# Spreading rows of cumulated decays over the partitions: transfers from DRAM in place of selecting matmuls, in a hybrid SSD and gated DeltaNet block

## The chip, the cores and the metric

The kernel runs on one core of one Trainium2 chip. The metric is the device time of one execution in microseconds. One execution was taken by the hardware profiler; all rows in this text come from that one. Engines are named as the profile names them: PE is the matmul engine, PEld its weight load, DVE the vector engine, ACT the scalar engine, POOL GpSimd, SP the sync engine, which here issues nearly all transfers (SPq is its sequencer).

## The reference, cut to what matters

One residual layer: an input projection feeds two token mixers (a Mamba-2 SSD and a gated DeltaNet), which are merged by gates and followed by a SwiGLU FFN. Both mixers work chunk by chunk and weigh pairs of tokens of a chunk by the decay between them:

```python
def segsum_exp(a_cum):
    l = a_cum.shape[-1]
    mask = jnp.tril(jnp.ones((l, l), dtype=bool))
    diff = a_cum[..., :, None] - a_cum[..., None, :]
    return jnp.exp(jnp.where(mask, diff, -jnp.inf))
...
scores = cb[:, :, :, None] * segsum_exp(a_cum)                           # SSD, 32 heads in 4 groups
qk = jnp.einsum("bchlk,bchsk->bchls", q, k) * decay                      # DeltaNet, 16 value heads
a_low = jnp.where(strict, jnp.einsum("bchlk,bchsk->bchls", k_beta, k) * decay, 0.0)
```

So for each head and chunk a square of exp(a_cum[l] - a_cum[s]) is wanted. The kernel works on 1040 tokens (16 meta tokens and 1024 others) in eight chunks of 128, and a ninth chunk, number 8, that holds the 16 meta tokens.

## The kernel before, in words

**Stages.** The norm and the first tiles of the projection come first (to about 105 us of the profile). Then eight DeltaNet subproblems of two value heads each run (to about 1090 us), then four SSD groups of eight heads (to about 1740 us), then the branch projections, the output projection and the FFN. While the mixers run, the PE also does the rest of the input projection: tiles of 128 columns by `dense` (L138, each step three matmuls on L141 to L143), with the weights loaded and split by `load_w` (L130). A tile that passes a convolution is copied to `raw` (L378); a gate or z tile is evacuated by ACT into `zt`, a tile with three buffers (L394, L408).

**The decays.** `cum` holds, with tokens on the partitions, the cumulated log decay of 48 heads (32 of the SSD, 16 of the DeltaNet). The square of a chunk needs the same numbers as a row that lies along the free dimension and is the same on all 128 partitions. The kernel makes it in two steps. At the start (L355 to L370) `cum` is transposed into `rr`, three copies of 32 heads below one another, and each copy is cut into three bfloat16 parts, which stand in `rowD` and `rowS`. Later `decay` (L416) does one matmul per head (L420): a column of the selecting matrix `selD` or `selS`, read by all output columns, times `row`, so that the three parts are added in PSUM on every partition. ACT then takes the difference to `cum` with a Relu per head (L423) and one Exp for all heads of the call (L426).

**Who calls it.** In a DeltaNet subproblem `i`, `dn_p1` (L501) runs for nine chunks: PE makes the product of the keys (L510), `decay` fills `E` for two heads, DVE masks the product (`kkm`, L513) and multiplies (L516) into `W`. After chunks 3 and 7 eight transfers each store `W` to `nd` (L523). `dn_inv` (L528) loads it as `X`, inverts it on DVE (L539, L541), stores and loads it again. `dn_merge` (L554, first matmuls L563) and `dn_p2` (L600) follow, chunk by chunk; `dn_p2` calls `decay` for a tile `E2`, which meets the PE again in L641. `E` and `E2` have two buffers each, from a pool with `bufs=2`. In the SSD, `ssd_chunk` (L690) calls `decay` twice for four heads, into tiles `Es` (three buffers) used by the matmuls of L748; each call has a PSUM bank of its own, of tag "p", from which ACT also takes `ec` (L733).

**What sets the order.** The kernel is written for a scheduler that puts each engine's instructions, SP's transfers among them, in an order of their readiness, with those that come earlier in the program first. It isn't the order of the program: in the profile matmuls of L141 to L143 stand between those of `dn_merge` and `dn_p2`. A tile of a tag waits for a buffer of that tag. The PSUM tag "p" has two banks; `dn_merge`, `dn_p1` and `ssd_chunk` take theirs from it.

Of the kernel before, what the change touches and what calls it, by code (L numbers as in the profile page):

```python
# [10 lines left out]
F32 = mybir.dt.float32  # L11
# [10 lines left out]
NM = 16  # L22
# [70 lines left out]
def body(tc, A):  # L93
# [77 lines left out]
    rs_dram = [dram.tile([8, 128], F32, name=f"rs_{g}") for g in range(NGRP)]  # L171
    nd_dram = [dram.tile([66, 32, 32], F32, name=f"nd_{i}") for i in range(NSUB)]
# [51 lines left out]
    rowS = tkp.tile([96, TT], BF16, name="rowS")  # L224
    rowD = tkp.tile([96, TT], BF16, name="rowD")
    selS = tkp.tile([96, 32], BF16, name="selS")
    selD = tkp.tile([96, 16], BF16, name="selD")
# [61 lines left out]
    with tc.tile_pool(name="dab", bufs=1) as sb:  # L289
# [4 lines left out]
        s0 = sb.tile([96, 48], F32, name="s0")  # L294
        sp.dma_start(s0, A["c_sel"])
        dve.tensor_copy(selS, s0[:, 0:32])
        dve.tensor_copy(selD, s0[:, 32:48])
# [57 lines left out]
        for row, h0 in ((rowD, 16), (rowS, 0)):  # L355
            c3 = sb.tile([128, 9, 3, 32], F32, name="c3")
            pool.tensor_copy(c3, cum[:, :, h0:h0 + 32].unsqueeze(2).broadcast_to([128, 9, 3, 32]))
            rr = sb.tile([96, TT], F32, name="rr")
            b2 = sb.tile([96, TT], BF16, name="b2")
            for c in range(9):  # L360
                c0, L = (NM + 128 * c, 128) if c < 8 else (0, NM)
                ps = psm("p")
                pe.transpose(ps[0:96, 0:L], V(c3[0:L, c], "p a b -> p (a b)"), ident[0:L, 0:L])
                act.copy(rr[:, c0:c0 + L], ps[0:96, 0:L])
            for i in range(3):
                r32 = slice(32 * i, 32 * i + 32)
                act.copy(row[r32], rr[r32])
                if i < 2:
                    dve.tensor_copy(b2, rr)
                    dve.tensor_tensor(rr, rr, b2, op=ALU.subtract)  # L370
# [44 lines left out]

    def decay(E, ps, row, sel, h0, hs, c):  # L416

        c0, L = cr(c)
        for i, h in enumerate(hs):
            pe.matmul(ps[0:L, 128 * i:128 * i + L], sel[:, h:h + 1].broadcast_to([96, L]),  # L420
                      row[:, c0:c0 + L], start=True, stop=True)
        for i, h in enumerate(hs):
            act.activation(E[0:L, i, 0:L], ps[0:L, 128 * i:128 * i + L], AF.Relu,  # L423
                           bias=cum[0:L, c, h0 + h:h0 + h + 1], scale=-1.0)
        n = len(hs)
        act.activation(E[0:L, 0:n, 0:L], E[0:L, 0:n, 0:L], AF.Exp, scale=-1.0)  # L426

# [73 lines left out]
    def dn_p1(i, c):  # L501
# [9 lines left out]
        decay(E, ps, rowD, selD, 32, (2 * i, 2 * i + 1), c)  # L511
# [88 lines left out]
    def dn_p2(i, c):  # L600
# [11 lines left out]
        decay(E, ps, rowD, selD, 32, (2 * i, 2 * i + 1), c)  # L612
# [77 lines left out]
    def ssd_chunk(g, c):  # L690
# [35 lines left out]
        E = [sb2.tile([128, 4, 128], F32, name="Es", bufs=3) for _ in range(2)]  # L726
        for q in range(2):
            pd = psm("p")
            decay(E[q], pd, rowS, selS, 0, range(8 * g + 4 * q, 8 * g + 4 * q + 4), c)
            pd = V(pd, "p (a b l) -> p a b l", a=2, b=2)  # L730
            for b in range(2):
                r = slice(64 * b, 64 * b + 64)
                act.activation(ec[r, 2 * q:2 * q + 2], pd[r, :, b], AF.Exp)  # L733
            dve.tensor_tensor(E[q], E[q], cbm.unsqueeze(1).broadcast_to([128, 4, 128]), op=ALU.mult)
# [439 lines left out]
def prepare(inp):  # L1174
# [46 lines left out]
    sel = z(96, 48)  # L1221
    for i in range(3):
        sel[32 * i:32 * i + 32, 0:32] = np.eye(32)
        sel[32 * i + 16:32 * i + 32, 32:48] = np.eye(16)
    d["c_sel"] = sel
    return d


# [11 lines left out]
```

## Time and profile before

| | us |
|---|---|
| median of 3 runs | 2960.96 |
| lowest and highest of them | 2960.52, 2972.54 |
| the profiled execution, its own time | 2960.07 |
| its span, first to last instruction | 2958.4 |
| mean granted clock of the PE | 0.99 of full |

The profile has a page with the busy time of each engine, the time that each group of instructions took, and the chain of work that ended last; the trace answers for single stretches, lines and tiles. Busy time of the PE is modelled for pipelined matmuls, so two matmuls that overlap can both be long: what one costs is the distance between the starts of its neighbours.

### The profile page before, as it was taken

The page shows a single profiled execution, that of the slowest core. Times are in us where ns is not written, and L with a number is a line of the kernel's source. Part 1 is how long each engine was busy: PE and PEld are TensorE (multiplying, and loading weights), DVE is VectorE, ACT ScalarE, POOL GpSimd, SP SyncE. Part 2 cuts the span into 40 slices and gives each one's busy share as a digit, 9 for nine tenths or more (in the row PEclk, how much of TensorE's full clock was granted, in tenths as well). Part 3 has the DMA queues.
Part 4 walks back from the last instruction along what each step waited for, and adds up shares of the span by engine and source line. Part 5 has one row for each costly group of instructions (what it writes and reads, how often), then busy time and mean ns, then how long its engine had stood idle before and what let it go on. Part 6 is the DMA issues. An engine that isn't in the chain of part 4 may idle for free.

```text
span 2958.4 us, 42844 instructions
## 1 busy us (share of the span) xinstructions
PE 2900.6 (98%) x16121; PEld 2442.0 (83%) x16121; DVE 1971.9 (67%) x3882; ACT 1293.4 (44%) x3240; POOL 184.8 (6%) x193
## 2 busy tenths in 40 slices
PE   8999999999999999999999999999997999999997
PEld 7888888888888889979888778888876788888886
DVE  7678687787786755767777753564768655556446
ACT  5645545546456353545555544122234233333213
POOL 1000000000000000000000000000101432230000
PEclk9999999999999999999999999999998999999998
DMA  3111121120111201011111124352442222226212
GB/s 114 51 51 44 41 61 44 37 65 27 53 58 30 93 29 51 30 67 47 51 45 45 68 76 154 106 178 90 135 160 86 102 83 86 86 85 224 90 54 75
DMA packets 119255, 227.33 MB, mean 77 GB/s; under 512 B 47064, under 2 KB 53880, under 8 KB 119048
## 3 DMA queue, kind: packets, MB, share of 16 engines
q1 hardware_dynamic: 117320, 222.50, 22.7%
q8 instruction: 127, 2.08, 0.3%
q10 hardware_dynamic: 1728, 2.10, 0.2%
q14 instruction: 80, 0.66, 0.1%
HBM read 175.16 MB, written 49.38 MB: 76 GB/s over the span
## 4 chain that ended last, share of the span: by engine, by line
PE 91%; DVE 4%; DMA 2%; issue 1%; ACT 1%; POOL 1%; SPq 0%; DVEq 0%; ACTq 0%; POOLq 0%
PE psd L142 16%; PE psd L141 16%; PE psd L143 16%; PE pq_p L1002 1%; PE pq_p L1003 1%; PE ps_o L748 1%; PE pq_p L1004 1%; PE ps_p L563 1%; PE pq_psd L1002 1%; PE ps_o L641 1%; PE ps_z L448 1%; PE pq_psd L1003 1%; PE pq_psd L1004 1%; PE ps_a L631 1%; PE ps_b L738 1%
## 5 line engine op out<-in xcount | busy, mean ns | idle before, releaser
L142 PE MATMUL psd<-u_lo,whi 128*128 128x512 f32 (+3 forms) x2136 | 766.2, 359 | 3.7 <-DVE u_lo L150 2.7
L141 PE MATMUL psd<-u_hi,whi 128*128 128x512 f32 (+3 forms) x2136 | 761.1, 356 | 0.0
L143 PE MATMUL psd<-u_hi,wlo 128*128 128x512 f32 (+3 forms) x2136 | 754.9, 354 | 0.7 <-DVE wlo L135 0.7
L134 ACT CAST whi<-wraw 128x1024 fp32r<-128x1024 f32 (+2 forms) x197 | 188.0, 954 | 634.8 <-PE psd L142 454.3
L142 PEld LDWEIGHTS psd<-u_lo,whi 128*128 128x128 f32 x2136 | 406.2, 190 | 40.5 <-issue 5.1
L143 PEld LDWEIGHTS psd<-u_hi,wlo 128*128 128x128 f32 x2136 | 403.9, 189 | 33.0 <-issue 3.3
L141 PEld LDWEIGHTS psd<-u_hi,whi 128*128 128x128 f32 x2136 | 402.6, 189 | 34.6 <-issue 4.2
L135 DVE TENSOR_TENSOR wlo<-wraw,whi 128x1024 fp32r<-128x1024 f32 (+2 forms) x197 | 217.8, 1106 | 138.8 <-ACT whi L134 129.5
L143 PE MATMUL psd<-blk,wlo 128*128 128x512 f32 x512 | 199.4, 389 | 0.8 <-DVE wlo L135 0.8
L141 PE MATMUL psd<-blk,whi 128*128 128x512 f32 x512 | 199.2, 389 | 0.0
L142 PE MATMUL psd<-blk,whi 128*128 128x512 f32 x512 | 199.2, 389 | 0.0
L143 PEld LDWEIGHTS psd<-blk,wlo 128*128 128x128 f32 x512 | 96.1, 188 | 21.6 <-DVE wlo L135 1.7
L141 PEld LDWEIGHTS psd<-blk,whi 128*128 128x128 f32 x512 | 96.1, 188 | 20.0
L142 PEld LDWEIGHTS psd<-blk,whi 128*128 128x128 f32 x512 | 96.1, 188 | 19.8
L908 DVE TENSOR_TENSOR part<-part,psd 128x512 f32<-128x512 f32 x96 | 65.5, 683 | 70.2 <-PE psd L143 70.2
L378 ACT COPY raw<-psd 128x256 f32<-128x256 f32 x165 | 73.4, 445 | 81.9 <-PE psd L143 80.1
L379 POOL MEMSET raw<- 128x3 f32 x56 | 6.3, 113 | 1393.0 <-DVE qk L384 537.1
L986 POOL TENSOR_TENSOR sw<-wraw 128x512 f32<-128x512 f32 x44 | 69.3, 1575 | 353.1 <-DMA wraw<-w_gu 345.1
L702 DVE TENSOR_TENSOR xdt<-ps_z,dtb 128x512 f32<-128x512 f32 (+1 forms) x36 | 24.8, 690 | 89.0 <-PE ps_z L699 89.0
L539 DVE TENSOR_TENSOR itmp<-X 66x30 f32<-66x30 f32 (+14 forms) x240 | 78.2, 326 | 6.3 <-DMA X<-nd 0.8
L541 DVE TENSOR_TENSOR X<-X,itmp 66x30 f32<-66x30 f32 (+14 forms) x240 | 78.3, 326 | 5.9
L423 ACT ACTIVATE Es<-ps_p,cum 128x128 f32<-128x128 f32 x256 | 75.4, 371 | 11.0 <-PE ps_p L420 10.9
(678 smaller groups left out, 6145.3 us busy)
## 6 DMA issues: line engine op xcount, KB each, us to landing
wraw<-w_in SPq DMA_DIRECT2D x105, 512.0 KB, 3.3
wraw<-w_gu SPq DMA_DIRECT2D x48, 512.0 KB, 3.3
wraw<-w_br SPq DMA_DIRECT2D x36, 512.0 KB, 3.4
c<-hc SPq DMA_DIRECT2D x22, 512.0 KB, 2.6
hc<-c SPq DMA_DIRECT2D x22, 512.0 KB, 5.7
wraw<-w_dn SPq DMA_DIRECT2D x40, 256.0 KB, 2.6
g<-zt SPq DMA_DIRECT2D x32, 256.0 KB, 2.0
y_d<-zt SPq DMA_DIRECT2D x32, 256.0 KB, 2.1
```

The lines of the kernel that those rows point to most:

```text
L134: act.copy(hi[:, 0:kk], raw[:, 0:kk])
L135: dve.tensor_tensor(lo[:, 0:kk], raw[:, 0:kk], hi[:, 0:kk], op=ALU.subtract)
L141: pe.matmul(ps[:, 0:n], hi[:, wk0 + k], ahi(k), start=(k == 0), stop=False)
L142: pe.matmul(ps[:, 0:n], hi[:, wk0 + k], alo(k), start=False, stop=False)
L143: pe.matmul(ps[:, 0:n], lo[:, wk0 + k], ahi(k), start=False, stop=(k == kk - 1))
L378: dense_u((name, lambda ps, p0, p1: act.copy(raw[:, 3 + p0:3 + p1], ps)))
L423: act.activation(E[0:L, i, 0:L], ps[0:L, 128 * i:128 * i + L], AF.Relu, bias=cum[0:L, c, h0 + h:h0 + h + 1], scale=-1.0)
L539: dve.tensor_tensor(t, X[:, 0:j, j:j + 1].broadcast_to([66, j, m]), X[:, j:j + 1, j + 1:32].broadcast_to([66, j, m]), op=ALU.mult)
L541: dve.tensor_tensor(X[:, 0:j, j + 1:32], X[:, 0:j, j + 1:32], t, op=ALU.add)
L908: dve.tensor_tensor(part[:, m, cs], part[:, m, cs], ps, op=ALU.add)
L986: pool.tensor_tensor(t, x, y, op=op)
L1002: pe.matmul(ps, w[0][:, k], y[0][:, k], start=start and k == 0, stop=False, skip_group_check=not start)
```

## The change

The rows are no longer made by matmuls. At the start `cum` is transposed once for all 48 heads (nine transposes of 48 columns in place of eighteen of 96), copied to `rr` by ACT, and stored to a DRAM tensor `cum_dram` by one transfer. The bfloat16 parts and the selecting matrices go. A new function `spread` issues one transfer on SP per call of `decay`: it reads `n` rows of a chunk from `cum_dram` and writes them to every partition of the decay tile. `decay` then works in place in SBUF, with the same Relu per head and the same Exp. In the SSD the two transfers are issued ahead, `ec` is taken from the decay tile before `decay` overwrites it, no PSUM bank of tag "p" is used for it, and `Es` has four buffers in place of three.

```diff
-        for row, h0 in ((rowD, 16), (rowS, 0)):
-            c3 = sb.tile([128, 9, 3, 32], F32, name="c3")
-            pool.tensor_copy(c3, cum[:, :, h0:h0 + 32].unsqueeze(2).broadcast_to([128, 9, 3, 32]))
-            rr = sb.tile([96, TT], F32, name="rr")
-            b2 = sb.tile([96, TT], BF16, name="b2")
-            for c in range(9):
...
-                pe.transpose(ps[0:96, 0:L], V(c3[0:L, c], "p a b -> p (a b)"), ident[0:L, 0:L])
-                act.copy(rr[:, c0:c0 + L], ps[0:96, 0:L])
-            for i in range(3):
-                r32 = slice(32 * i, 32 * i + 32)
-                act.copy(row[r32], rr[r32])
-                if i < 2:
-                    dve.tensor_copy(b2, rr)
-                    dve.tensor_tensor(rr, rr, b2, op=ALU.subtract)
+        rr = sb.tile([48, TT], F32, name="rr")
+        for c in range(9):
...
+            pe.transpose(ps[0:48, 0:L], cum[0:L, c], ident[0:L, 0:L])
+            act.copy(rr[:, c0:c0 + L], ps[0:48, 0:L])
+        sp.dma_start(cum_dram, rr)
...
-    def decay(E, ps, row, sel, h0, hs, c):
+    def spread(E, h0, n, c):
 
         c0, L = cr(c)
-        for i, h in enumerate(hs):
-            pe.matmul(ps[0:L, 128 * i:128 * i + L], sel[:, h:h + 1].broadcast_to([96, L]),
-                      row[:, c0:c0 + L], start=True, stop=True)
-        for i, h in enumerate(hs):
-            act.activation(E[0:L, i, 0:L], ps[0:L, 128 * i:128 * i + L], AF.Relu,
-                           bias=cum[0:L, c, h0 + h:h0 + h + 1], scale=-1.0)
-        n = len(hs)
+        sp.dma_start(E[0:L, 0:n, 0:L], cum_dram[h0:h0 + n, c0:c0 + L].unsqueeze(0).broadcast_to([L, n, L]))
+
+    def decay(E, h0, n, c):
+
+        c0, L = cr(c)
+        for i in range(n):
+            act.activation(E[0:L, i, 0:L], E[0:L, i, 0:L], AF.Relu, bias=cum[0:L, c, h0 + i:h0 + i + 1], scale=-1.0)
         act.activation(E[0:L, 0:n, 0:L], E[0:L, 0:n, 0:L], AF.Exp, scale=-1.0)
...
-        decay(E, ps, rowD, selD, 32, (2 * i, 2 * i + 1), c)
+        spread(E, 32 + 2 * i, 2, c)
+        decay(E, 32 + 2 * i, 2, c)
...
-        E = [sb2.tile([128, 4, 128], F32, name="Es", bufs=3) for _ in range(2)]
+        E = [sb2.tile([128, 4, 128], F32, name="Es", bufs=4) for _ in range(2)]
         for q in range(2):
-            pd = psm("p")
-            decay(E[q], pd, rowS, selS, 0, range(8 * g + 4 * q, 8 * g + 4 * q + 4), c)
-            pd = V(pd, "p (a b l) -> p a b l", a=2, b=2)
+            spread(E[q], 8 * g + 4 * q, 4, c)
+        for q in range(2):
+            pd = V(E[q], "p (a b) l -> p a b l", b=2)
             for b in range(2):
                 r = slice(64 * b, 64 * b + 64)
                 act.activation(ec[r, 2 * q:2 * q + 2], pd[r, :, b], AF.Exp)
+            decay(E[q], 8 * g + 4 * q, 4, c)
             dve.tensor_tensor(E[q], E[q], cbm.unsqueeze(1).broadcast_to([128, 4, 128]), op=ALU.mult)
```

## Rows read from the trace of the kernel before

**Rows 1.** The page, busy time, share of the span and instructions by engine.
```profile
PE 2900.6 (98%) x16121; PEld 2442.0 (83%) x16121; DVE 1971.9 (67%) x3882; ACT 1293.4 (44%) x3240; POOL 184.8 (6%) x193
```

**Rows 2.** The page, shares of the span in the chain that ended last.
```profile
PE 91%; DVE 4%; DMA 2%; issue 1%; ACT 1%; POOL 1%; SPq 0%; DVEq 0%; ACTq 0%; POOLq 0%
```

**Rows 3.** Stretches: length, busy us (count) by engine, granted clock, DMA share, GB/s.
```profile
370.00:434.00 64.00, 63.88 (x387) 56.94 (x386) 57.88 (x135) 27.96 (x74) 1.40 (x5) 1.00 0.24 70
434.00:490.00 56.00, 56.00 (x412) 45.10 (x411) 38.92 (x136) 39.04 (x154) 0.10 (x1) 1.00 0.07 18
...
1190.00:1330.00 140.00, 140.00 (x861) 116.92 (x860) 101.43 (x165) 75.54 (x176) 0.51 (x5) 1.00 0.15 52
```

**Rows 4.** The same view of line 141 alone, its PE and PEld time.
```profile
434.00:490.00 56.00, 8.22 (x20) 3.60 (x19) 1.00 0.07 18
```

**Rows 5.** Line 420: count, ns min/median/max, first and last start us.
```profile
L420 PE MATMUL ps_p<-rowS,selS x256: 216/218/232, 1189.1 to 1734.1; 96*128 96x128 bf16 x128
L420 PE MATMUL ps_p<-rowD,selD x144: 169/217/222, 96.5 to 984.4; 96*128 96x128 bf16 x128, 96*16 96x16 bf16 x16
L420 PE MATMUL ps_b<-rowD,selD x128: 217/221/314, 105.4 to 1076.8; 96*128 96x128 bf16 x128
```

**Rows 6.** PE in order of time, SSD: start us, us, line, tiles, count.
```profile
1330.33 0.39 PE L420 MATMUL ps_p<-rowS,selS 96*128 96x128 bf16 x4
1330.56 1.11 PE L738 MATMUL ps_b<-Ct,Ss 128*128 128x128 f32 x8
...
1333.14 0.40 PE L142 MATMUL psd<-u_lo,whi 128*128 128x512 f32 x1
1333.37 0.40 PE L143 MATMUL psd<-u_hi,wlo 128*128 128x512 f32 x1
1333.69 0.38 PE L420 MATMUL ps_p<-rowS,selS 96*128 96x128 bf16 x4
1333.89 0.48 PE L141 MATMUL psd<-u_hi,whi 128*128 128x512 f32 x1
1334.20 0.40 PE L142 MATMUL psd<-u_lo,whi 128*128 128x512 f32 x1
```

**Rows 7.** PE in order of time, DeltaNet, around one pair of L420.
```profile
245.75 0.28 PE L420 MATMUL ps_p<-rowD,selD 96*128 96x128 bf16 x2
245.84 0.42 PE L141 MATMUL psd<-u_hi,whi 128*128 128x384 f32 x1
```

**Rows 8.** Groups by line and shape: busy us, mean ns, idle before by releaser.
```profile
L426 ACT ACTIVATE E<-E 128x256 f32<-128x256 f32 x128 | 53.6, 420 | 2.4
...
L423 ACT ACTIVATE E<-ps_p,cum 128x128 f32<-128x128 f32 x128 | 41.3, 367 | 12.5 <-PE ps_p L420 4.4 <-DVE W L516 3.0 <-DVE f L662 1.7
...
L516 DVE SCALAR_TENSOR_TENSOR W<-E,w,kkm 128x128 f32<-128x128 f32 x128 | 39.8, 344 | 2.0 <-ACT E L426 0.8
L651 ACT ACTIVATE oq<-v 128x128 f32<-128x128 f32 x128 | 37.9, 299 | 9.1 <-DVE v L647 7.2 <-DVE rrr L162 1.8
L449 ACT ACTIVATE ps_z<-ps_z 128x128 f32<-128x128 f32 x128 | 33.9, 265 | 32.1 <-PE ps_z L448 31.8
```

**Rows 9.** Transfers: count, KB each, median us to landing; last, all of rst.
```profile
nd<-W SPq DMA_DIRECT2D x128, 16.0 KB, 1.5
X<-nd SPq DMA_DIRECT2D x8, 256.0 KB, 3.7
...
rst<-rs SPq DMA_DIRECT2D x4, 512.0 KB, 5.9
...
DMA to landing us min/median/max: 4.6/5.9/5.9
```

**Rows 10.** SP in order of time, fifth subproblem: start us, us, transfer, count.
```profile
603.10 8.61 SPq L523 DMA_DIRECT2D nd<-W  x16
```

**Rows 11.** Line 516 between 580 and 725 us, the fifth subproblem's decays used.
```profile
L516 DVE SCALAR_TENSOR_TENSOR W<-E,w,kkm x16: 341/346/352, 596.4 to 608.2; 128x128 f32<-128x128 f32 x16
```

**Rows 12.** Line 641 between 434 and 490 us, eight chunks of one subproblem.
```profile
L641 PE MATMUL ps_o<-v,E x32: 270/275/377, 444.3 to 489.6; 128*128 128x128 f32 x32
```

More of the change, by code (lines that the diff above doesn't have):

```diff
@@ L171, in body @@
     rs_dram = [dram.tile([8, 128], F32, name=f"rs_{g}") for g in range(NGRP)]
+    cum_dram = dram.tile([48, TT], F32, name="cum_d")
     nd_dram = [dram.tile([66, 32, 32], F32, name=f"nd_{i}") for i in range(NSUB)]
@@ L223, in body @@
     dte = tkp.tile([128, 9, 48], F32, name="dte")
[L224 to L227, printed above, removed]
     convp = tkp.tile([128, len(CONV), 5], F32, name="convp")
@@ L293, in body @@
         dve.tensor_scalar(dnw, dnw, 0.5, None, op0=ALU.mult)
[L294 to L297, printed above, removed]
         alog = sb.tile([128, 48], F32, name="alog")
@@ L352, in body @@
         act.activation(dte, lastb, AF.Exp)
-        for row, h0 in ((rowD, 16), (rowS, 0)):
-            c3 = sb.tile([128, 9, 3, 32], F32, name="c3")
-            pool.tensor_copy(c3, cum[:, :, h0:h0 + 32].unsqueeze(2).broadcast_to([128, 9, 3, 32]))
-            rr = sb.tile([96, TT], F32, name="rr")
-            b2 = sb.tile([96, TT], BF16, name="b2")
-            for c in range(9):
-                c0, L = (NM + 128 * c, 128) if c < 8 else (0, NM)
-                ps = psm("p")
-                pe.transpose(ps[0:96, 0:L], V(c3[0:L, c], "p a b -> p (a b)"), ident[0:L, 0:L])
-                act.copy(rr[:, c0:c0 + L], ps[0:96, 0:L])
-            for i in range(3):
-                r32 = slice(32 * i, 32 * i + 32)
-                act.copy(row[r32], rr[r32])
-                if i < 2:
-                    dve.tensor_copy(b2, rr)
-                    dve.tensor_tensor(rr, rr, b2, op=ALU.subtract)
+        rr = sb.tile([48, TT], F32, name="rr")
+        for c in range(9):
+            c0, L = (NM + 128 * c, 128) if c < 8 else (0, NM)
+            ps = psm("p")
+            pe.transpose(ps[0:48, 0:L], cum[0:L, c], ident[0:L, 0:L])
+            act.copy(rr[:, c0:c0 + L], ps[0:48, 0:L])
+        sp.dma_start(cum_dram, rr)
     def conv_tile(name, out, raw=None):
@@ L611, in dn_p2 @@
         pe.transpose(ps[:, 384:512], kT, ident)
-        decay(E, ps, rowD, selD, 32, (2 * i, 2 * i + 1), c)
+        spread(E, 32 + 2 * i, 2, c)
+        decay(E, 32 + 2 * i, 2, c)
         qkm = sb.tile([128, 128], F32, name="qkm")
@@ L1220, in prepare @@
     d["c_stri"] = np.triu(np.ones((128, 128), np.float32), 1)
[L1221 to L1225, printed above, removed]
     return d
```

## The prediction

> **What bounds the kernel now.** I read the page's busy times first. The PE is busy for 2900.6 us, 98% of the span; DVE stands at 67%, ACT at 44% [rows 1]. Then the chain that ended last: the PE holds 91% of it, transfers 2% [rows 2]. So work taken from the PE is the likeliest to come back as time, and new transfers touch something that now hardly ends anything. Third, the stretches, since a mean over stages could hide others. In the SSD stretch from 1190 to 1330 us the PE has no idle time at all, and in the two DeltaNet stretches, 370 to 434 and 434 to 490, it is idle for 0.12 and 0.00 us [rows 3]. These two differ, though. In the first, in which one subproblem is inverted and the next convolutions run, DVE is busy for 57.88 of 64 us. In the second, in which `dn_merge` and `dn_p2` run, DVE has 38.92 of 56, and the PE spends only 20 steps (of three matmuls each) on the projection [rows 4]; the rest are small matmuls of a chain that goes from PE to ACT to DVE and back. There a busy PE is also a PE that fills the waits of a chain with projection work that happens to be ready. That is where this change can lose what it saves.
>
> The Trainium skill, Perfetto Trace Analysis, section Identifying the Most-Contended Engine, says that matmul busy time is a bad measure of the PE's load and that the share of LDWEIGHTS is a better one. This trace has 83% there [rows 1], so by that rule the PE has some slack, and part of the matmul time removed would not come back; the first rival below is that case.
>
> **What is removed from the PE.** 256 selecting matmuls of the SSD, 144 of `dn_p1` and 128 of `dn_p2`, 528 in all [rows 5]. Their median durations of 217 to 221 ns overlap and are not their price. The price is the distance between starts. Four in a train of small matmuls: from 1330.33 to 1330.56, 0.23 us. Four between projection matmuls: from the start of L143 at 1333.37 to that of L142 at 1334.20 are 0.83 us, in which two projection matmuls would take 2 x 0.23 (1333.14 to 1333.37), so 0.36 us [rows 6]. There are 64 fours in the SSD: 64 x 0.23 = 14.7 at least, 64 x 0.36 = 23.0 at most; both kinds are frequent, so I take 0.29 each, 18.6 us. In the DeltaNet they come in pairs, 136 of them. One pair takes 0.09 us from its start to the next projection matmul [rows 7]; half of a four in a train would be 0.115. I take 0.10: 13.6 us, with bounds of 0.09 and 0.12, 12.2 to 16.3. Nine fewer transposes at the start, at the 0.06 us that one of four takes in a train, give 0.5 us. Sum: 18.6 + 13.6 + 0.5 = 32.7 us less work on the PE, with bounds of 27 and 40.
>
> The start also loses bfloat16 casts and subtractions on ACT and DVE. I count them at nothing: the rows were ready at 96.5 us, when the first selecting matmul ran [rows 5], and what fills the time is the PE's projection work. For the same reason I count the new store of `cum_dram` and the wait of the first `spread` for it at nothing; both lie beside the projection.
>
> **What is added on ACT.** The Relu now reads SBUF. The nearest rows are one function, Square with accumulation, on 128x128: 265 ns from PSUM, 299 from SBUF [rows 8]. So 34 ns for each of 528 Relus and 128 `ec`s: 22 us over 1600 us. ACT is busy for 39.04 of 56 and 75.54 of 140 us [rows 3], so this is covered; if it weren't, it would lie on the chunk's chain with 0.1 us per chunk.
>
> **What is added on SP and the transfers.** 136 transfers of 128 KB (eight of them 16-wide) and 64 of 256 KB. No row shows one of this size that spreads rows over partitions. The nearest is `rst`, the same form with 512 KB: 4.6 to 5.9 us to landing. Below lies the 16 KB of `nd` with 1.5, beside it the 256 KB of `X` with 3.7 [rows 9]. A line between `nd` and `rst` gives 2.2 to 2.5 us for 128 KB and 3.0 to 3.6 for 256 KB. I take 2.4 and 3.3, with 1.5 and 3.7 as bounds for the first. The transfer waits for a buffer, so what matters is how far ahead it is issued.
>
> In the SSD, `Es` has four buffers, two chunks. The selecting matmuls of 32 chunks run from 1189.1 to 1734.1 us [rows 5], 17 us a chunk. A buffer comes free when a chunk's L748 is over, so the transfer for the chunk after the next has some 17 us, and needs 3.3, or 5.9 for both together. Hidden. SP's stores of `zt` and the weight loads are queued on the same engine: a `spread` that waits for its buffer delays the weight load behind it. But a load goes into the second of two `wraw` buffers, a whole tile ahead, so I count this at nothing. If that cover were gone, each transfer would cost its 3.3 us, 64 x 3.3 = 211 us in all; with 17 us a chunk nothing points that way.
>
> In `dn_p2`, the 32 matmuls on `E2` of eight chunks start between 444.3 and 489.6 us [rows 12], 5.7 us a chunk. The transfer for chunk c is issued when L641 of chunk c-2 is over, so 11 us remain. It needs 2.4 + 2 x 0.37 + 0.42 for Relus and Exp [rows 8], and some 0.4 on DVE: 4 us. Hidden.
>
> In `dn_p1` it is not. Two buffers of `E` come free by L516 of DVE, and the chunks follow one another closely: sixteen L516 of eight chunks start within 596.4 to 608.2 us [rows 11], 1.5 us a chunk, 13.7 us for nine. After the change the two first chunks are loaded early, since their buffers have long been free. The other seven go in two alternating lanes, at most four rounds one after the other. A round is the transfer, two Relus, the Exp and two L516: 2.4 + 0.73 + 0.42 + 0.69 = 4.2 us [rows 8]. Four make 17 us. The eight stores of `W` after chunk 3 hold SP for half of 8.61 us [rows 10], and the `spread` of chunk 5, free at the same moment, waits behind them: 4.3 more. So 21 us in place of 13.7 plus its start, about 6 us longer. With 1.5 us to landing and the spreads ahead of the stores it is 13 us, no longer than now; with 3.7 and the stores 26 us, 12.6 longer. Below nothing isn't expected: the first two chunks start a little earlier, but a lane can't be faster than its round.
>
> What of it ends up in the time? `dn_p1` is followed by the stores, `dn_inv` and `dn_merge`, one chain per subproblem; the PE goes on with the projection meanwhile. Its reserve: `zt` has three buffers, so three halves of eight steps, 24, can be run ahead of `dn_p2`'s end, and 20 are used now [rows 4]. The four left are twelve matmuls of 0.23, 2.8 us of cover. A second cover is in `dn_inv`: DVE works there on convolutions in between (57.88 of 64 us [rows 3]), and a later inversion finds more of these done; I put this at 2 us. So 6 - 2.8 - 2 = 1.2 us uncovered, for seven subproblems (the first waits for the start anyway): 8 us.
>
> **The sum.** Against the profiled execution, 2960.07 us, which is 0.9 below the median of the runs shown (too little to matter here): 2960 - 33 + 8 = 2935 us, a gain of 0.8%. Its own bounds are 2922 (40 saved, little lost) and 2946 (27 saved, 1.9 us uncovered per subproblem).
>
> **The rivals.**
> - *The chain, not the PE, bounds the DeltaNet.* Then the 13.6 us saved there don't come back, since the PE's small matmuls only fill a chain, and DVE gives no cover: 6 - 2.8 = 3.2 us for seven subproblems, 22 us. 2960 - 19 + 22 = 2963, no change. For it: only 20 projection steps in 56 us [rows 4] and PEld's 83%. Against it: idle PE time is nil in both stretches [rows 3].
> - *Slower, by the rounds of `dn_p1`.* A transfer that lands after 3.7 us makes the nine chunks 12.6 us longer. The reserve covers 2.8, the rest delays the inversion: 9.8 x 7 = 69 us. 2960 - 33 + 69 = 2996. It decides from the point at which the uncovered part of a subproblem passes 33 / 7 = 4.7 us. For it: X takes 3.7 us [rows 9], and weight loads share the queue. Against it: this stretch moves little, with a DMA share of 0.24 and 0.07 [rows 3].
> - *More gain.* The selecting matmuls cost 0.36 and 0.12 everywhere and nothing is lost: 2960 - 40 = 2920. For it: `dn_p1` and the SSD hold PSUM banks of tag "p" for a shorter time. Against it: four in a train cost 0.23 [rows 6].
>
> **How the numbers follow.** The forecast gets 0.60, no change 0.22, slower 0.13, more gain 0.05. The likeliest is 2935. The range from 2920 to 2978 holds the forecast, the first rival and the end of more gain; it leaves out the slower one and a little beyond. A measurement of this kernel can tell about 0.5%, 15 us, from no change. Faster by more than that: 0.60 + 0.05 = 0.65; within: 0.22; slower: 0.13.
>
> **What would show it.** Right: line 420 gone and the count of PE matmuls down by about 540; the SSD stage shorter by about 18 us with the PE still without idle time; the chain of the end with hardly any transfer of `cum`; landing near 2.4 and 3.3 us. For the loss: the span of L516 in a subproblem, 12 us now, near 18, and PE idle time of some 1 us before `dn_merge` or L641. Wrong: ACT waits at L423 for transfers in the SSD, PE idle time at L748, weight loads that come late behind a `spread`, or a span of L516 that passes 22 us.

## The result: slower by 4%, and the profile after

| | before | after |
|---|---|---|
| median, us | 2961.86 (4 runs, 2960.52 to 2972.54) | 3081.36 (4 runs, 3077.11 to 3088.74) |
| ratio, 95% interval | | 1.040, 1.037 to 1.043 |
| profiled execution, its span, us | 2960.07, 2958.4 | 3082.38, 3080.5 |
| DeltaNet, us (from 105 us to the end of its last L641 / L627) | 984.1 | 1050.4 |
| SSD, us (from there to the end of its last L748 / L735) | 649.0 | 707.2 |
| rest, us | 1220.3 | 1217.9 |

The forecast was a gain of 26 us; the change lost 120. Two stages lost it, 66 and 58 us; the rest, which the change doesn't touch, stayed. The split between the two is not clean: in its longer DeltaNet stage the PE also did projection work that before was left to the SSD stage (next rows). In the code of after the numbers are: `spread` L403, Relu L409, Exp L410 (before L423, L426), the products of `dn_p1` L501 (L516), `ec` L719 (L733), the matmuls on `Es` L735 (L748), those on `E2` L627 (L641).

The page of after: busy times and the chain that ended last, which answer to [rows 1, 2], then two groups (busy, mean ns, idle before and its releaser).

```profile
PE 2911.3 (95%) x15584; PEld 2440.1 (79%) x15584; DVE 1966.6 (64%) x3872; ACT 1314.0 (43%) x3225; POOL 178.6 (6%) x191
...
PE 75%; DMA 10%; ACT 7%; DVE 5%; issue 3%; POOL 0%; SPq 0%; DVEq 0%; ACTq 0%; POOLq 0%
...
L409 ACT ACTIVATE E<-E,cum 128x128 f32<-128x128 f32 (+1 forms) x272 | 94.8, 389 | 66.9 <-DMA E<-cum_d 65.8
L719 ACT ACTIVATE ec<-Es 64x256 f32<-64x256 f32 x128 | 52.9, 413 | 153.6 <-DMA Es<-cum_d 152.0
```

The PE has 537 matmuls fewer (528 selecting ones and nine transposes) and yet is busy for 10.7 us more. Transfers, 2% of the chain before, are 10% of it now, and ACT stood for 152.0 us before `ec` and 65.8 us before Relus of the DeltaNet until rows had landed. So the forecast's sign that something is wrong, waits of ACT for transfers in the SSD, is there. The three stages of after and then of before (length, busy us and count of PE, PEld, DVE, ACT, POOL, then the granted clock, DMA share, GB/s):

```profile
105.00:1155.00 1050.00, 997.80 (x6138) 838.58 (x6137) 739.36 (x2061) 533.09 (x1736) 10.09 (x41) 0.97 0.24 62
1155.00:1863.00 708.00, 644.51 (x3737) 554.28 (x3736) 461.89 (x751) 352.54 (x752) 2.21 (x22) 0.96 0.33 70
1863.00:3080.00 1217.00, 1173.93 (x5207) 967.69 (x5205) 689.46 (x962) 367.58 (x592) 148.84 (x102) 0.98 0.34 112
```

```profile
105.00:1089.00 984.00, 982.57 (x6336) 832.49 (x6336) 739.83 (x2061) 528.25 (x1772) 11.53 (x46) 0.99 0.16 49
1089.00:1738.00 649.00, 648.81 (x4078) 561.01 (x4076) 459.03 (x752) 336.18 (x756) 2.23 (x22) 1.00 0.15 52
1738.00:2958.00 1220.00, 1174.06 (x5210) 968.12 (x5208) 689.18 (x963) 367.72 (x592) 151.63 (x102) 0.98 0.33 112
```

The PE is now idle for 52 of 1050 us and 63 of 708 us, where it had been idle for 1.4 and 0.2. And the clock that it was granted fell from 0.99 to 0.97 and from 1.00 to 0.96. Leaving out the 268 and 256 selecting matmuls that stood in these stages, it ran 70 more in the DeltaNet stage and 85 fewer in the SSD stage.

**One chunk of the SSD, after.** ACT in order of time (start us, us, line, tiles, count, idle before), one answer:

```profile
1249.42 1.08 ACT L367 ACTIVATE raw<-Bt 128x1040 f32<-128x1040 f32 x1 [2.32 <-DVE Bt L366]
1252.41 0.48 ACT L362 COPY raw<-psd 128x384 f32<-128x384 f32 x1 [1.91 <-PE psd L143]
1256.86 0.86 ACT L719 ACTIVATE ec<-Es 64x256 f32<-64x256 f32 x2 [3.97 <-DMA Es<-cum_d]
1257.74 1.28 ACT L409 ACTIVATE Es<-Es,cum 128x128 f32<-128x128 f32 x4
...
1260.02 0.47 ACT L362 COPY raw<-psd 128x400 f32<-128x400 f32 x1
1260.39 1.05 ACT L134 CAST whi<-wraw 128x1024 fp32r<-128x1024 f32 x1
1261.34 1.25 ACT L364 ACTIVATE xt<-raw,convp 128x1040 f32<-128x1040 f32 x1
1262.49 0.25 ACT L695 CAST Bh<-ps_p 128x128 fp32r<-128x128 f32 x1
1262.64 0.62 ACT L146 CAST xh<-xde 128x512 fp32r<-128x512 f32 x1
```

SP, DVE (two lines) and PE in the same view, each from its own answer:

```profile
1251.87 2.60 SPq L403 DMA_DIRECT2D Es<-cum_d  x2
```

```profile
1258.72 0.69 DVE L689 TENSOR_TENSOR xde<-xdt,dte 128x512 f32<-128x512 f32 x1
...
1287.45 0.69 DVE L721 TENSOR_TENSOR Es<-Es,cbm 128x512 f32<-128x512 f32 x1
```

```profile
1260.69 0.27 PE L142 MATMUL psd<-u_lo,whi 128*128 128x256 f32 x1
1263.31 0.50 PE L701 MATMUL ps_a<-xh,Bh 128*128 128x512 f32 x1 [2.35 <-ACT xh L146]
```

The first of a chunk's two transfers is issued at 1251.87 us, as soon as L735 has released its buffer. ACT is through with what comes earlier in its order at 1252.89 and stands before `ec` until 1256.86. The result of all this, the decay, is first multiplied on DVE at 1287.45, 30 us later: there was no hurry. But behind `ec` and its Relus stand, in ACT's order, a copy of `raw`, a weight cast and at last `xh` of the chunk that the PE is at. DVE has finished `xde`, of which `xh` is made, at 1259.41, but ACT comes to it only at 1262.64. The PE works off what it has, and stands idle from 1260.96 to 1263.31 for `xh`. The Trainium skill, PSUM — Partial Sum Buffer, section Engine vs sequencer instructions, says that ScalarE's queue is strictly first in, first out; these rows agree.

What an idle PE costs further is in the windows of the same stretch (columns as above):

```profile
1250.00:1257.30 7.30, 7.30 (x50) 6.45 (x49) 5.60 (x11) 1.40 (x3) 0.10 (x1) 1.00 0.40 52
1257.30:1263.30 6.00, 3.66 (x32) 3.42 (x30) 3.82 (x5) 5.91 (x13) 0.00 (x0) 1.00 0.16 28
1263.30:1268.70 5.40, 5.39 (x24) 5.25 (x25) 4.05 (x6) 3.53 (x8) 0.00 (x0) 0.68 0.30 97
1268.70:1277.30 8.60, 8.60 (x58) 7.65 (x57) 5.47 (x10) 0.48 (x1) 0.10 (x1) 1.00 0.34 40
```

After the idle 2.35 us the granted clock is 0.68 over the next 5.4 us, partly at the lower of its two levels (1.2 GHz), and full again behind that. What that costs is seen in matmuls of one shape: two projection matmuls of 384 columns start 0.32 us apart in the slow stretch (1265.25 and 1265.57) and 0.18 us apart behind it (1269.17 and 1269.35).

**One subproblem of `dn_p1`, after.** DVE, SP and ACT in order of time, the third subproblem (other lines between left out; L603 is DVE's work on `E2`, which the profile names `E` too):

```profile
375.15 0.61 DVE L501 SCALAR_TENSOR_TENSOR W<-E,w,kkm 128x128 f32<-128x128 f32 x2
375.79 9.06 SPq L403 DMA_DIRECT2D E<-cum_d  x5
...
380.69 0.99 ACT L409 ACTIVATE E<-E,cum 128x128 f32<-128x128 f32 x3 [0.69 <-DMA E<-cum_d]
382.08 0.71 ACT L410 ACTIVATE E<-E 128x256 f32<-128x256 f32 x2
382.51 0.42 DVE L603 TENSOR_TENSOR E<-E,qkm 128x256 f32<-128x256 f32 x1 [1.73 <-ACT E L410]
382.69 0.69 ACT L409 ACTIVATE E<-E,cum 128x128 f32<-128x128 f32 x2
383.82 0.61 DVE L501 SCALAR_TENSOR_TENSOR W<-E,w,kkm 128x128 f32<-128x128 f32 x2
```

The round from one pair of L501 to the pair that uses the same buffer (another pair, of the other buffer, lies between) takes 383.82 - 375.15 = 8.7 us, where the forecast had 4.2. The span of L501 in the fifth subproblem, the counterpart of [rows 11]:

```profile
L501 DVE SCALAR_TENSOR_TENSOR W<-E,w,kkm x16: 341/346/352, 635.5 to 664.6; 128x128 f32<-128x128 f32 x16
```

It is 29 us, 12 before; over all eight subproblems, with chunk 8, it lies between 27.5 and 32.5 us.

### The profile page after: what moved, and what is told of

The parts are those of the page before. It is cut to its first block, busy times and chain, and to the rows that moved or that the text cites. A ratio compares the mean times of both kernels' runs of the same rounds, so it can differ in the third digit from the quotient of the medians.

```text
span 3080.5 us, 41985 instructions
## 1 busy us (share of the span) xinstructions
PE 2911.3 (95%) x15584; PEld 2440.1 (79%) x15584; DVE 1966.6 (64%) x3872; ACT 1314.0 (43%) x3225; POOL 178.6 (6%) x191
## 2 busy tenths in 40 slices
DMA packets 188197, 261.05 MB, mean 85 GB/s; under 512 B 50424, under 2 KB 122776, under 8 KB 187992
## 4 chain that ended last, share of the span: by engine, by line
PE 75%; DMA 10%; ACT 7%; DVE 5%; issue 3%; POOL 0%; SPq 0%; DVEq 0%; ACTq 0%; POOLq 0%
PE psd L141 13%; PE psd L142 13%; PE psd L143 13%; DMA Es<-cum_d 5%; DMA E<-cum_d 4%; ACT Es L409 1%; PE pq_p L989 1%; PE pq_p L990 1%; PE pq_p L991 1%; PE pq_psd L990 1%; PE pq_psd L989 1%; PE pq_psd L991 1%; PE ps_p L548 1%; PE ps_o L627 1%; ACT E L409 1%
## 5 line engine op out<-in xcount | busy, mean ns | idle before, releaser
L141 PE MATMUL psd<-u_hi,whi 128*128 128x512 f32 (+3 forms) x2136 | 772.1, 362 | 12.2 <-ACT raw L362 11.8
L143 PE MATMUL psd<-u_hi,wlo 128*128 128x512 f32 (+3 forms) x2136 | 767.7, 360 | 0.7 <-DVE wlo L135 0.7
L141 PEld LDWEIGHTS psd<-u_hi,whi 128*128 128x128 f32 x2136 | 411.3, 193 | 55.2 <-ACT raw L362 14.6
L143 PEld LDWEIGHTS psd<-u_hi,wlo 128*128 128x128 f32 x2136 | 411.5, 193 | 37.3 <-issue 3.1
L409 ACT ACTIVATE E<-E,cum 128x128 f32<-128x128 f32 (+1 forms) x272 | 94.8, 389 | 66.9 <-DMA E<-cum_d 65.8
L719 ACT ACTIVATE ec<-Es 64x256 f32<-64x256 f32 x128 | 52.9, 413 | 153.6 <-DMA Es<-cum_d 152.0
L409 ACT ACTIVATE Es<-Es,cum 128x128 f32<-128x128 f32 x256 | 84.2, 392 | 1.5
```

The costliest lines, as they stand in the source:

```text
L141: pe.matmul(ps[:, 0:n], hi[:, wk0 + k], ahi(k), start=(k == 0), stop=False)
L143: pe.matmul(ps[:, 0:n], lo[:, wk0 + k], ahi(k), start=False, stop=(k == kk - 1))
L409: act.activation(E[0:L, i, 0:L], E[0:L, i, 0:L], AF.Relu, bias=cum[0:L, c, h0 + i:h0 + i + 1], scale=-1.0)
```

## The experiments

The theory after the result (A): the time goes where ACT, in its order, stands behind rows that are issued late, because their target is freed late. The rivals at first: (B) the loss comes from what stays when the transfers are gone, Relus that read SBUF, PSUM banks taken otherwise or another order; (C) the traffic, that is ports and queues, slows the other work. From raw on B stands for the cost of the transfers themselves, wherever their data go, and D for SP's queue. All runs in one table; stage lengths and PE times from the same windows as above, times of one run unless an interval stands. The kernel before gave 2971.57 beside the first four, a median of 2969.73 (7 runs) beside raw, late and bufs, 2964.30 (17) beside best1, ssd_late and before_late, and 2966.44 (7) beside best2. Its runs lie between 2955.53 and 2978.89 us, with a mean granted clock of 0.992 to 0.983, so some 20 us between two single runs say little by themselves. Nor do 8 us of the DeltaNet stage: its code is that of before in before, ssd_only, ssd_late and before_late, and took 980.4 to 988.3 us there.

| kernel | us | DeltaNet: length, PE idle | SSD: length, PE idle | ratio to before |
|---|---|---|---|---|
| before | 2961.86 | 984.1, 1.4 | 649.0, 0.2 | |
| after | 3081.36 | 1050.4, 52.2 | 707.2, 63.5 | 1.040 (1.037 to 1.043) |
| no_transfer | 2913.84 | 959.2, 5.6 | 628.5, 0.2 | |
| unwaited | 2939.89 | 982.9, 24.9 | 632.2, 0.1 | |
| dn_only | 2997.67 | 1041.0, 43.7 | 633.3, 0.3 | |
| ssd_only | 3031.00 | 980.4, 0.2 | 726.4, 67.4 | |
| raw | 2999.84 | 998.5, 23.9 | 677.1, 42.8 | 1.010 (1.007 to 1.014) |
| late | 2987.17 | 1047.0, 50.2 | 618.8, 1.6 | |
| bufs | 3020.77 | 985.0, 24.6 | 710.6, 53.4 | |
| best1 | 2938.41 | 984.4, 18.0 | 636.6, 1.4 | 0.991 (0.988 to 0.993) |
| ssd_late | 2936.66 | 982.9, 0.2 | 634.5, 1.9 | 0.989 (0.986 to 0.993) |
| before_late | 2960.83 | 988.3, 1.2 | 650.2, 1.0 | 1.000 (0.997 to 1.002) |
| best2 | 2935.39 | 980.9, 16.9 | 639.2, 1.5 | 0.988 (0.985 to 0.992) |

**no_transfer** and **unwaited**: what the matmuls were worth, and what the traffic costs.

```diff
 # no_transfer: spread returns without a transfer; Relu and ec read a constant tile
-            act.activation(E[0:L, i, 0:L], E[0:L, i, 0:L], AF.Relu, bias=cum[0:L, c, h0 + i:h0 + i + 1], scale=-1.0)
+            act.activation(E[0:L, i, 0:L], ones[0:L, 0:L], AF.Relu, bias=cum[0:L, c, h0 + i:h0 + i + 1], scale=-1.0)
 # unwaited: the same, but every transfer is issued, into a tile of its own that one element on POOL reads
+        Ed = sb.tile([128, 2, 128], F32, name="Ed")
+        spread(Ed, 32 + 2 * i, 2, c)
+        pool.tensor_tensor(scr, Ed[0:1, 0, 0:1], E[0:1, 0, 0:1], op=ALU.mult)
```

> The changed kernel with the 200 transfers of rows left out: the Relus and the Exps for ec read a constant tile, so the decays are those of constant rows; everything else is done. Theory A (the loss is the engines' wait for transfers that are issued only when a decay tile comes free): without them ACT has nothing to wait for, so the 33 us that the matmuls cost come back whole: 2925 to 2940 us, and ACT never waits for cum_d. Theory B (the loss comes from what stays: Relus that read SBUF, PSUM banks taken otherwise, another order of the instructions): about 3080 us as in the changed kernel, at least over 2990.

> The same kernel without waits, but the 200 transfers are issued into tiles of their own, which only a one-element operation on POOL reads, once the decays of the chunk are done; the decays are again those of constant rows. So SP and the queue carry all the traffic, and ACT, DVE and PE wait for none of it. Theory A: within 10 us of the kernel without transfers, 2925 to 2950 us. Theory C (the loss is traffic: SP busy issuing, weight loads behind the spreads, engines of the queue shared): near the changed kernel, over 3030 us.

Measured: 2913.84 us without transfers, below the range of theory A. The span is 46 us below that of the profiled run of before (the run of before beside it was 58 above). The two stages give 24.9 and 20.5 us back, and their PE is as good as never idle. So B falls, the PE was the bound, and the matmuls cost more than 33 us, not less. With the traffic, but without its waits (unwaited), the SSD is 3.7 us longer and the DeltaNet 23.7; the whole is inside its range of 2925 to 2950, but 26 us from no_transfer and not within 10. The second number says little on traffic, because the operation on POOL also reads `E`, and so `E` comes free only after a transfer; in the SSD 64 transfers of 256 KB, 16 MB, cost some 4 us when nobody stands waiting. Of the 168 us between the spans of no_transfer and after no more than 26 are traffic by this run, which leaves little of C.

**dn_only** and **ssd_only**: each half of the change by itself, the other keeps its selecting matmuls.

> Only the DeltaNet takes its rows by transfers; the SSD keeps its selecting matmuls (both preparations stand at the start). By the traces the last L641 of the DeltaNet moved from 1089 to 1155 us and the rest of the loss, some 60 us, lies in the SSD. Theory A: each part loses by itself, so 3015 to 3035 us here, with the sixteen multiplications by the decays of a subproblem spread over about 30 us as in the changed kernel. Theory C or any joint cause (both kinds of transfer on the queue): well under 3010.

> Only the SSD takes its rows by transfers; the DeltaNet keeps its selecting matmuls. Theory A: the SSD's part of the loss, 3010 to 3030 us, with ACT waiting some 150 us in all for Es. If the two parts don't add up to the 120 us of the whole change, one of them depends on the other.

Measured: the spans are longer than that of before by 37.5 and 70.8 us; together 108 of the 122 us that the whole change costs. So both halves lose by themselves. ssd_only is 1 us above its range. dn_only missed: it lies 17 us below its range, under the 3010 that the expectation gave to a joint cause. Its rows tell why without one: its DeltaNet stage lost 57 us, near the 66 of after, and its SSD stage, whose code is that of before, came out 15.7 us shorter, with 88 matmuls fewer on the PE (3990 and 4078), which the longer stage ahead had let it do. In the other direction, ssd_only's SSD stage, with no such help, lost 77 us, not 58. The largest waits of ACT, from the view of waits (us in total, times, longest), first ssd_only, then dn_only:

```profile
ACT ec L750 <- DMA Es<-cum_d: 158.3, 32, 9.8
```

```profile
ACT E L433 <- DMA E<-cum_d: 70.6, 63, 6.9
```

**raw**, **late**, **bufs**: the same transfers, with one change each to when they are issued or when ACT comes to them.

```diff
 # raw: rows land in a tile of their own, freed by ACT; Es has three buffers then
-        spread(E, 32 + 2 * i, 2, c)
-        decay(E, 32 + 2 * i, 2, c)
+        Ra = sb.tile([128, 2, 128], F32, name="Ra", bufs=2)
+        spread(Ra, 32 + 2 * i, 2, c)
+        decay(E, Ra, 32 + 2 * i, 2, c)
 # late: only the SSD; bias of ec and Relu from a tile that depends on the chunk's own xdt
+        dve.scalar_tensor_tensor(cl[:, 0:8], xdt[:, 0:8], 0.0, cum[:, c, hs], op0=ALU.mult, op1=ALU.add)
+        dve.tensor_scalar(cl[:, 8:9], xdt[:, 0:1], 0.0, None, op0=ALU.mult)
-                act.activation(ec[r, 2 * q:2 * q + 2], pd[r, :, b], AF.Exp)
+                act.activation(ec[r, 2 * q:2 * q + 2], pd[r, :, b], AF.Exp, bias=cl[r, 8:9])
 # bufs
-        E = sb.tile([128, 2, 128], F32, name="E")
+        E = sb.tile([128, 2, 128], F32, name="E", bufs=6)
-        E = [sb2.tile([128, 4, 128], F32, name="Es", bufs=4) for _ in range(2)]
+        E = [sb2.tile([128, 4, 128], F32, name="Es", bufs=5) for _ in range(2)]
```

> The change with one thing altered: the transfer no longer writes into the decay tile itself but into a tile of its own for the raw rows (DeltaNet: two buffers for dn_p1, two for dn_p2; SSD: two, one chunk), and the Relu reads it and writes the decay tile. The raw tile comes free when ACT has read it, not when PE or DVE has used the decay, so the next transfer is issued up to a chunk earlier. The transfers, their number and size, and the work of every engine stay the same. Theory A (the loss is ACT, which works in order, standing behind a transfer that is issued late because its target is freed late): the waits of ACT for cum_dram, 152 us in the SSD and 66 us in the DeltaNet, fall below 20 and 25 us, the spans of L501's counterpart in a subproblem go from 30 us to under 24, and the time comes to 2925 to 2950 us, near the kernel with dummy targets (2940). Theory B (the transfers themselves, their small packets and their contention, cost the time wherever their data go): ACT still waits over 100 us, and the time stays above 3040. Theory D (SP's queue, not the buffer, delays them: stores and loads that stand ahead): waits halve at most, time about 3010.

> The change with the buffers as they are, but in the SSD the ec and Relu instructions of a chunk get their bias from a small tile that DVE computes from that chunk's own xdt (cum plus zero times xdt; two more small DVE operations per chunk). So these ACT instructions are ready only when the chunk begins, and stand later in ACT's queue, when the rows have long landed. The DeltaNet is left as changed. Theory A (the place in ACT's order is what costs): ACT's wait for Es falls from 152 to under 20 us, the SSD stage (707 us) comes back to 630 to 655 us, and the whole to 3005 to 3030 us, since DeltaNet's loss stays. Theory B (the rows' transfers cost the time by themselves): the SSD stays at some 700 us and the whole at 3070 or above. A third outcome: ACT then waits at the same place for xdt instead, no gain, 3060 to 3090.

> The change with more buffers for the decay tile and nothing else: six for dn_p1's E in place of two, five for the SSD's Es in place of four (more don't fit). Six remove nearly all of the rounds of dn_p1; the fifth Es lets one of a chunk's two tiles be loaded a chunk earlier, the other still waits for py of two chunks before, now beside the 3 us of ACT work on the first. Theory A: the spans of the L501 products go from 30 us to 15 to 20, the DeltaNet from 1050 us to about 975 to 1000; ACT's wait in the SSD from 152 to 40 to 70 us and its stage from 707 to 660 to 685; the whole 2970 to 3010 us. If the rounds are set by something else than the buffer (SP's queue, or ACT's own order), the spans stay above 25 us and the DeltaNet above 1030.

*raw* came to 2999.84 us, 82 us better than the change and still slower than before. ACT's waits halved, to 76.2 and 27.2 us; theory A had said under 20 and 25 (the spans of the products in `dn_p1`, 18.6 to 23.8 us, are as it said). Time and waits are the figures of rival D, though these rows, in which SP issues at once, don't show its mechanism. SP and ACT of raw, two answers:

```profile
1298.04 2.06 SPq L403 DMA_DIRECT2D Er<-cum_d  x2
```

```profile
1296.73 1.57 ACT L409 ACTIVATE Es<-Er,cum 128x128 f32<-128x128 f32 x5 [1.80 <-PE ps_o L738]
...
1298.73 0.97 ACT L409 ACTIVATE Es<-Er,cum 128x128 f32<-128x128 f32 x3
1300.02 0.60 ACT L393 ACTIVATE zt<-psd 128x512 f32<-128x512 f32 x1 [0.32 <-PE psd L143]
1300.51 0.62 ACT L410 ACTIVATE Es<-Es 128x512 f32<-128x512 f32 x1
1302.72 0.84 ACT L722 ACTIVATE ec<-Er 64x256 f32<-64x256 f32 x2 [1.59 <-DMA Er<-cum_d]
```

Four Relus empty the raw tile, SP issues at once, and the next thing that ACT does with these rows is 4.7 us behind the issue, again just behind the transfer. Issued a chunk earlier, the rows are also asked for a chunk earlier. (The three buffers of `Es` add a wait that isn't of the transfers: 41.3 us before Relus, for the matmuls that still read the tile.) So theory A as I had put it (the buffer comes free too late) was only half of it: the transfer's lead over ACT doesn't grow with the buffer, since ACT's order follows the transfer.

*late* shows the other half. No transfer is issued earlier, but ACT's instructions can't be ready before their chunk begins. ACT's wait for `Es` is gone altogether:

```profile
L722 ACT ACTIVATE ec<-Es,cl x128: 490/504/512, 1244.4 to 1766.2; 64x256 f32<-64x256 f32 x128
L722 ACTq EVENT_SEMAPHORE  x28: 17/17/17, 1258.8 to 1762.1; - x28
its engine sat idle before it (us, times) until:
  DVE cl L717: 3.6, 3
```

The SSD took 618.8 us in place of 707.2, with its PE idle for 1.6 us and its clock granted in full (1.00). Stage and whole are below their ranges (630 to 655, 3005 to 3030). Some of that gain is work that the longer DeltaNet had already done: the PE runs 3746 matmuls in this stage, 3826 in that of no_transfer. The DeltaNet, left as it was, still lost 63 us.

*bufs* missed in one stage and hit in the other. In the SSD a fifth buffer does nothing: 710.6 us and 139.9 us of waits. In the DeltaNet six buffers of `E` end the rounds; the span of L501 in the fifth subproblem, and the waits:

```profile
L501 DVE SCALAR_TENSOR_TENSOR W<-E,w,kkm x16: 329/343/347, 594.8 to 605.8; 128x128 f32<-128x128 f32 x16
```

```profile
ACT ec L719 <- DMA Es<-cum_d: 139.9, 32, 6.8
ACT E L409 <- DMA E<-cum_d: 70.3, 53, 6.2
```

11 us from the first to the last L501, in place of 29, and the DeltaNet goes from 1050 to 985 us, as long as before. So its 66 us were the rounds of `dn_p1`. The whole, 3020.77, is above its range. ACT's 70 us of waits are as many as they were, and the PE is still idle for 24.6 us, about what the matmuls had given back.

**best1**, **ssd_late**, **before_late**, **best2**: put together, with controls.

```diff
 # ssd_late: ssd_only with late's bias; before_late: the kernel before with late's bias
 # best1: late, and in the DeltaNet
+        E = sb.tile([128, 2, 128], F32, name="E", bufs=4)
+        Rb = sb.tile([128, 2, 128], F32, name="Rb", bufs=2)
+        spread(Rb, 32 + 2 * i, 2, c)
+        decay(E, 32 + 2 * i, 2, c, rows=Rb)
 # best2: late, E with bufs=6, and in dn_p2 a bias that depends on v2 of the chunk before
+            dve.scalar_tensor_tensor(cd, d["v2"][:, 0, 0:2], 0.0, cum[:, c, 32 + 2 * i:34 + 2 * i],
+                                     op0=ALU.mult, op1=ALU.add)
+        decay(E, 32 + 2 * i, 2, c, cd)
```

> The change with its two kinds of stall taken out by what the runs before suggest: in the SSD the bias of ec and Relu comes from a small DVE tile that depends on the chunk's own xdt, as in the kernel late; in the DeltaNet dn_p1's E has four buffers in place of two, and dn_p2's rows land in a raw tile of their own (two buffers), which the Relu reads. All transfers stay. Theory A (ACT stands in order behind rows that are issued late): DeltaNet 970 to 990 us, SSD 615 to 635 us, ACT's waits for cum_dram under 25 us in all, the whole 2910 to 2940 us, faster than the kernel before. Theory B (traffic and SP's queue cost DeltaNet time whatever the buffers): DeltaNet stays above 1000 us, the whole 2945 to 2965, no gain.

> The SSD part of the change alone (the DeltaNet keeps its selecting matmuls), with the late bias of the kernel late. Theory A: the 71 us that the SSD part lost turn into a gain, since the place in ACT's order was all that was wrong: SSD 615 to 635 us in place of 649 before, DeltaNet 980 to 985 as before, the whole 2925 to 2945 us. If the gain that the kernel late showed in the SSD stage (619 us) came from work that DeltaNet's stalls had let the PE do earlier, the SSD stays at 640 to 650 and the whole at 2950 to 2962.

> A control: the kernel before, with its selecting matmuls, and nothing but the late bias in the SSD (two small DVE operations per chunk more). Theory A: the bias only repairs a wait that this kernel doesn't have, so the time stays within 0.5% of the kernel before, 2950 to 2975 us, SSD 640 to 655. Rival: the later order is better in itself, SSD 615 to 635 us and 2925 to 2945 us; then late's gain is not one of the transfers.

> All transfers of the change; the SSD with the late bias; dn_p1's E with six buffers; and in dn_p2 the same idea as in the SSD: the bias of its Relus comes from a tile of two columns that DVE computes from v2 of the chunk before (cum plus zero times v2), so ACT takes them nearly a chunk after the transfer was issued. Theory A (the place in ACT's order costs, in the DeltaNet as well): ACT's waits for cum_dram, 71 us in bufs and 47 in best1, fall under 20 us, the DeltaNet from 984 to 960 to 975 us, the whole to 2905 to 2928 us. Rival (in the DeltaNet the loss is not ACT's place but the chain of a chunk, to which the late Relus are added): the waits go and the DeltaNet stays at 980 or above, the whole 2935 or above.

*ssd_late* is the cleanest. With nothing changed against ssd_only but when ACT may start (and two small DVE operations a chunk for it), 3031 us become 2936.66, 1.1% faster than before; the SSD is 14.5 us shorter than before, at the same DeltaNet, so this gain isn't borrowed from the stage ahead. *before_late* shows that the later bias is no improvement by itself: 1.000. *best1* and *best2* keep all transfers and come to the same time as ssd_late. In the DeltaNet ACT's waits are down from 70 to 47 and 29 us, but the stage stays at 984 and 981 us; the expectation for best2 (960 to 975) failed, and time and stage are the figures of its rival, the chain of a chunk, though 29 us of waits are left. best1 too has more waits than its 25 us, and an SSD stage 2 us above its range. So the DeltaNet's transfers could be made harmless, not useful. best2's DeltaNet is 21.7 us longer than that of no_transfer. Its PE is idle for 17 us there and not 6, which makes 11; the other 10 are the clock, 0.983 in place of 0.993 over the stage. A clock that much lower comes and goes between runs of the kernel before, so it needn't be the transfers'. What holds the 11 us is open: waits of ACT that are left, the added small operations, or the chain of a chunk.

That the place in ACT's order decides in the SSD is shown by late and ssd_late. Why the order puts these instructions right behind their transfer is argued only: the kernel's order goes by readiness, and an order that takes a transfer for shorter than the 5 us measured here would do just that.

## Why the prediction was wrong, point by point

**What bounds the kernel: right.** Taking the matmuls away with nothing in their place gave 46 us. The Trainium skill's rule (Perfetto Trace Analysis, Identifying the Most-Contended Engine), by which the share of LDWEIGHTS, 83%, leaves the PE some slack, would have had part of the saving lost; no_transfer shows all of it and more come back, with that share about unchanged (809.65 of 959 us in the DeltaNet, 84%; 832.49 of 984, 85%, before). So the trace doesn't agree with that use of the rule. What the Trainium skill says there is meant for how near a kernel is to the roofline, which no run here tests.

**The matmuls' price: under-sized.** In the SSD 20.5 us against 18.6 taken, within its bounds of 14.7 to 23.0. In the DeltaNet 24.9 against 13.6, beyond the bound of 16.3 (21 by the shortest of the four stages with the code of before): a pair costs up to 24.9 / 134 = 0.19 us, not 0.10 (two of the 136 pairs lie before the stage). Part of it may be 18 other matmuls that left the stretch (6336 - 6050 - 268), at most some 6 us by an estimate at 0.36 us, the mean busy time of a projection matmul; with the shortest stage and these 6 us it would be 15 and within the bound. If the rest is the matmuls', the distance between two starts on the PE misses something there; what, wasn't tried.

**ACT's cost of reading SBUF: small and covered, as forecast.** A Relu takes 392 ns in the SSD and 371 before, `ec` 413 and 379.

**The transfers: under-sized.** Taken were 3.3 us for 256 KB and 2.4 for 128 KB. On the chain of after the pieces of the two kinds, the first in the SSD and the last in the DeltaNet, are (start us, us):

```profile
1251.87 4.91 DMA Es<-cum_d
...
1272.28 5.04 DMA Es<-cum_d
```

```profile
506.18 3.05 DMA E<-cum_d
513.08 3.18 DMA E<-cum_d
```

From issue to ACT's release it is 5 us for the first of two transfers of 256 KB (mean of the 26 long pieces of the SSD 5.4) and 3.4 for 128 KB (37 pieces); on the chain stand only those that something waited for. The two of a chunk don't slow each other: in the chunk shown the second is issued at 1254.09, and its packets run from 1256.07 to 1259.38, behind those of the first (1252.90 to 1256.12). The line through `nd` and `rst` gave too little. What differs from `rst` may be the size of the pieces: packets went from 119255 to 188197 for the whole kernel, 68942 more, and the 32 MB of the spreads in pieces of 512 bytes are 65536. No run varied that size, so this cause is argued. The Trainium skill, DMA: Bandwidth & Descriptors, section Anatomy of one DMA, has a fit for transfers that GpSimd issues, 2.0 us and the bytes at 436 KB per us; an estimate by it is 2.3 and 2.6 us for these sizes, and the measured means are 1.1 and 2.8 us above.

**"Hidden" in the SSD: the step that failed, 58 us.** The working took the transfer (3.3 us, or 5.9 for both) as hidden in the 17 us until the decay is used. The transfers did land in time for that, 30 us ahead of it. What it left out is where the reader of the rows stands in its own queue. ACT comes to it 1 us after the issue, not when the decay is needed, stands there for 4 us until the rows have landed, and all that ACT has for other work waits behind it. The check on what it would cost "if that cover were gone" (64 x 3.3 = 211 us) named the price and then turned it down; ACT's waits were 152 us, and the stage paid 58 of them net of the 20.5 saved, so 79. With the work that the longer DeltaNet took over left in the stage (ssd_only) it paid 77 net, so 98.

**"Hidden" in `dn_p2`: failed in the same way, at a smaller price.** With the rounds of `dn_p1` gone (bufs) ACT still waits 70 us; the later bias in `dn_p2`, the DeltaNet's only difference between bufs and best2, takes 41 of them away, and the PE's idle time falls from 24.6 to 16.9 us. So some 8 us of idle time; the stage itself came out 4 us shorter, which is within the spread of one code's stage (8 us), so this price is not shown clear of noise.

**The rounds of `dn_p1`: the mechanism was right, the size wrong, 66 us.** In the round shown a lane takes 8.7 us rather than 4.2: 3 to 4 us for the transfer, and in the rest ACT and DVE serve `E` and `E2` of two subproblems' work in turn, as the rows show. The span became 27.5 to 32.5 us, beyond the 26 of the upper bound and well past the 22 named as a sign of error. And the 4.8 us of cover did not nearly meet it: the sum had 8 us of loss for seven subproblems, and six buffers took away 65. The rival "slower" had this mechanism and a price of 69 us. It got 0.13, against it stood "this stretch moves little", which says nothing on how long one transfer takes.

**What no step had: the clock.** The same 9875 matmuls kept the PE busy for 997.8 + 644.5 = 1642 us in the first two stages after, and 953.5 + 628.8 = 1582 us in no_transfer (9876). Of the 168 us between the two kernels, 110 are PE idle time, and some 60 are the PE working slower; the granted clock accounts for some 50 of these, since 0.97 and 0.96 of the two stages after are 60 us short of full speed, and the 0.993 and 1.00 of no_transfer 7. So here the waits of the engine that feeds the PE were paid once as a wait and about half again in clock. It isn't so for every pause: the 24.9 us of idle time in unwaited's DeltaNet went with a clock of 0.99.

**And the number.** 2935 us is what the repaired kernels take: 2935 to 2938, 1.1% below before. The agreement is luck: the matmuls gave back 45 us in the two stages and not 32; best1 and best2, which keep all transfers, lose 22 to 25 of them again in the DeltaNet and 8 to 11 in the SSD, not the 8 of the sum; and ssd_late leaves the DeltaNet's matmuls where they were. The saving was forecast for a kernel whose transfers don't stall ACT; this one's do.

## What to carry to other kernels

Whether a transfer is hidden was not settled here by the time from its issue to the use of the result. It was settled at the first instruction that waits for it, on an engine that works in order: ask how far behind the issue that instruction stands in its queue, and what stands behind it. The Trainium skill's advice (DMA: Bandwidth & Descriptors, Rules for kernel authors) to issue early and wait late has two halves; raw did the first and won 30 of the SSD's 58 us, late and ssd_late did the second and won all of them. And a tile that is loaded, worked on in place and used has one buffer for three phases: give the loop that runs fastest as many buffers as its round is long.

## What the runs showed of the hardware

A spread of rows over 128 partitions in runs of 512 bytes takes 3.4 us for 128 KB and 5.4 us for 256 KB from issue to use (means over the chain of after), while 64 of the larger kind made the SSD 3.7 us longer as long as nobody stood waiting (unwaited against no_transfer, one run each). A pause of the PE of 2.35 us was followed by 5.4 us at a granted clock of 0.68.
